# A two-layer diffusion step in one kernel: the opening's scale and shift vectors from TensorE in column groups, six tiles from the scaled, un-normalised input

## The chip, the core and the metric

The kernel runs on one core of a Trainium2 chip. Its engines work side by side, each on its own queue of instructions in order: TensorE (PE in the profile; its weight loads are PEld), VectorE (DVE), ScalarE (ACT), GpSimd (POOL) and SyncE (SP), which issues the loads. Transfers are carried by 16 DMA engines. The metric is the device time of one execution in microseconds; the median of several runs is compared.

## The reference

One inference step of a two-layer backbone over 384 tokens of width 1024: 128 context tokens (modulated by `c_ctx`) and 256 latent tokens (modulated by `c`). Each layer is a half-step SwiGLU FFN, a token mixer (layer 0: a bidirectional recurrent block, layer 1: grouped-query attention) and a second half-step FFN. Each of these reads a normalised and modulated input. What the change touches is the input of the very first FFN:

```python
def rmsnorm(x, g):
    y = xf * lax.rsqrt(jnp.mean(xf * xf, axis=-1, keepdims=True) + EPS)
    return (y * g).astype(x.dtype)

def modulation(cvec, w, b):
    m = jax.nn.silu(cvec) @ w + b
    return m.reshape(cvec.shape[0], N_SUB, 3, D_MODEL)

def sub_in(x, g, m, sidx):
    shift, scale = m[:, sidx, 0], m[:, sidx, 1]
    return rmsnorm(x, g[sidx]) * (1 + scale[:, None, :]) + shift[:, None, :]

def swiglu(h, w_gu, w_down):
    gt, up = jnp.split(h @ w_gu, 2, axis=-1)
    return (jax.nn.silu(gt) * up) @ w_down
...
xs = xs + 0.5 * sub_gate(ms, 0) * swiglu(sub_in(xs, g, ms, 0), ffn_w_gu[layer, 0], ffn_w_down[layer, 0])
```

Since the norm's factor is one number per token, `(x * r * G + S) @ W` equals `r * ((x * G) @ W) + S @ W`, with `G = (1 + scale) * g` and `S` the shift. A product can therefore start from `x * G` without the norm, if `S @ W` is computed beside it and `r` is multiplied in afterwards.

## The kernel before

**Layout.** Activations lie transposed: 8 blocks (k = 0 to 7) of 128 features on the partitions, 384 tokens along the row (128 context, then 256 latent). Each float32 operand is split into a high part (a rounded copy, `hi`, usually made on ScalarE, line 162) and a low part (the rest, `lo`, made on VectorE, line 163), and each product is three matmuls: hi by hi, hi by lo, lo by hi (`mm3`, lines 173 to 178). `hh` and `hl` (lines 101 to 103) hold the two parts of the current input, with two more columns 384 and 385 (`N:NB`) for the two shift vectors; `ALL` is 384 columns, `AUG` 386. A weight tile is 128 output features by all 1024 inputs, 512 KB, and takes 8 x 3 matmuls.

**Later sub-layers** already use the identity above: `pre` writes `x * G`, `shift_cols` writes the shift columns, `head` runs six tiles on 386 columns, and `ev` in `ffn` (lines 400 to 412) multiplies the norm `R` in and adds the shift product taken from columns 384 and 385. Then `hgen` (line 313) writes the truly normalised input for the other tiles.

**The opening** (`start`, line 993) is the exception. It loads the small constants and the input `X`, spreads the two conditioning vectors over all partitions with eight matmul instructions (line 1016) into `sb`, squares `X` for the norm's statistics (`square`, line 270), and loads for each k the scale tile (`sc`), the shift tile (`sh`) and one of six gate/up weight tiles (`GUP`). All of these loads are issued from SP. Then a list of tokens, `SPROG` (line 68), writes out the order of the work:

- `A`: the scale vector of k = 0 and the statistics; `N`: the norm, spread into `R` (`norm_end`).
- `S`k: the shift of k < 6 on TensorE: eight matmuls against `sT` (two columns) into two PSUM rows, and a copy of them to `row` (lines 1037 to 1045). `T`k: a turn of that row into a column, by a small matmul, and its bias on ScalarE. For k = 6 and 7 the shift is computed by two dots on VectorE instead (`mod_dot`, line 196: one pass over 128x1024 elements for each conditioning vector).
- `H`k (`gen`): the scale of k by two dots on VectorE, then `hgen`, the normalised input of block k.
- `P`k (`step`): the matmuls that block k makes possible for the six tiles, on 384 columns.

Three things fix the order. All matmuls of `start` that go through its `mm` are chained ("pe"), so TensorE takes them in the order of SPROG. On VectorE the dots and the low parts of the six weight tiles are chained ("fill"); other operations are placed by a scheduler where it finds room. And in a pool of buffers a load waits until the buffer before it is free: `mc` (scale and shift tiles) has 12, `gr` (the six raw weight tiles) 6, `raw` (later weights) 3.

After `start`, `ffn` evacuates the six tiles in three pairs (`evac`, line 394), and goes on with ordinary tiles (`plain`, line 379, whose matmuls appear at lines 175 to 177) on the normalised input. These are not chained.

Of the kernel before, what the change touches and what calls it, by code (L numbers as in the profile page):

```python
# [37 lines left out]
MP = 0  # L38
# [24 lines left out]
XO = [slice(0, 4), slice(4, 8)]  # L63
SHP = 6
CP = ()
GUP = (0, 1, 2, 3, 4, 5)
PB = True
SPROG = "A S0 N S1 T0 H0 S2 T1 H1 P0 S3 T2 H2 P1 S4 T3 H3 P2 S5 T4 H4 P3 T5 H5 P4 P5 T6 H6 T7 H7 P6 P7"
# [18 lines left out]
class Net:  # L87
# [98 lines left out]
    def mod_pe(self, l, n):  # L186
        nc = self.nc
        raw = self.wp.tile([P, 1024], F32, tag="raw", name="raw", bufs=3)
        nc.sync.dma_start(raw, self.a["mod_w"][l, n])
        ps = self.misc()  # L190
        for k in range(KD):
            nc.tensor.matmul(ps[:, :2], lhsT=raw[:, k * P:(k + 1) * P], rhs=self.sT[:, k, :], start=k == 0, stop=k == KD - 1)
        st, k = divmod(n, KD)
        nc.vector.tensor_copy(self.mod[l, st // 3, st % 3][:, k, :], ps[:, :2])

# [91 lines left out]
    def stats(self):  # L287
        nc = self.nc
        ps = self.misc()
        st = ps[:, N:]  # L290
        for i in range(3):
            c = slice(i * P, (i + 1) * P)
            self.chain("pe", nc.tensor.matmul(st[:, i:i + 1], lhsT=self.acc[:, c], rhs=self.ones[:, 0:1], start=True, stop=True))
        self.nps, self.ny = ps, self.rstd(st[:, :3], 3, 1.0 / D)
# [90 lines left out]
    def ffn(self, l, s, fills, nxt, banks=None, hp=3, begun=None, prep=False):  # L385
# [607 lines left out]
    def start(self, B=6):  # L993
# [3 lines left out]
        sh, sc = {}, {}  # L997
        row = {}
        one = T_([P, KD], F32, name="one")
        if PB:  # L1000
            cr = self.fp.tile([P, 1024], F32, tag="junk", name="junk", bufs=1)[0:2, :]
            sel = T_([2, 2, P], F32, name="sel")
            nc.sync.dma_start(cr, a["cv"])
            nc.sync.dma_start(sel, a["sel"])
# [6 lines left out]
        if PB:
            nc.scalar.activation(cr, cr, AF.Silu)
            for v in range(2):
                for c in (slice(0, 512), slice(512, 1024)):
                    b = self.bank()
                    nc.tensor.matmul(b, lhsT=sel[:, v, :], rhs=cr[:, c], start=True, stop=True)
                    nc.scalar.activation(self.sb[:, v, c], b, AF.Copy)
        else:
            self.load_cond()
        for k in range(KD):  # L1020
            self.square(k)
        nc.vector.tensor_scalar(out=one, in0=self.sm("mod_b", KD, KD), scalar1=1.0, scalar2=None, op0=ALU.add)
        los = []
        banks = [self.bank() for _ in range(B)]
        tr = self.bank()
        tiles = []
        for k in range(KD):
            for o, dst in ((KD, sc), (0, sh)):
                dst[k] = T_([P, D], F32, tag="mc", name="mc", bufs=12)
                nc.sync.dma_start(dst[k], a["mod_w"][0, o + k])  # L1030
            for _ in range(GUP.count(k)):
                tiles.append(self.gu_tile(0, 0, len(tiles), T_([P, D], F32, tag="gr", name="gr", bufs=B)))
                los.append(self.wlo)
        self.last["pe"] = None
        S, G = self.mod[0, 0, 0], self.mod[0, 0, 1]

        def shift(k, src=None):
            if src is None:
                if k >= SHP:
                    return  # L1040
                src = sh[k]
            for j in range(KD):
                mm(tr[0:2, :P], lhsT=self.sT[:, j, :], rhs=src[:, j * P:(j + 1) * P], start=j == 0, stop=j == KD - 1)
            row[k] = T_([2, P], F32, tag="row", name="row", bufs=3)
            nc.scalar.activation(row[k], tr[0:2, :P], AF.Copy)

        def turn(k):
            if k >= SHP:
                self.mod_dot(0, k, sh[k])
                nc.vector.tensor_scalar(out=S[:, k, :], in0=S[:, k, :], scalar1=self.sm("mod_b", k, 1), scalar2=None, op0=ALU.add)  # L1050
                return
            mm(tn[:, 2 * k:2 * k + 2], lhsT=row[k], rhs=self.ident[0:2, 0:2], start=True, stop=True)
            nc.scalar.activation(S[:, k, :], tn[:, 2 * k:2 * k + 2], AF.Identity, bias=self.sm("mod_b", k, 1))

        def scale(k):
            if k in CP:
                return
            self.mod_dot(0, KD + k, sc[k])
            scale_end(k, G[:, k, :])

        def scale_pe(k):
            mm(tn[:, 64 + 2 * k:64 + 2 * k + 2], lhsT=row[k], rhs=self.ident[0:2, 0:2], start=True, stop=True)
            scale_end(k, tn[:, 64 + 2 * k:64 + 2 * k + 2])

        def scale_end(k, src):
            g = self.sm("norm_g", k, 1).to_broadcast([P, 2])
            nc.vector.scalar_tensor_tensor(out=G[:, k, :], in0=src, scalar=one[:, k:k + 1], in1=g, op0=ALU.add, op1=ALU.mult)
# [13 lines left out]
        def gen(k):  # L1081
            if k:
                scale(k)
            for i in range(B):
                if GUP[i] == k:
                    self.chain("fill", los[i])
            keep = self.last["fill"]
            self.hgen(0, 0, k)
            self.last["fill"] = keep

        def first():
            self.last["fill"] = None
            scale(0)
            self.stats()

        def second():
            self.norm_end()
            self.last["fill"] = self.dg

        tn = None  # L1100
        for tok in SPROG.split():
            k = int(tok[1:] or 0)
            if tok[0] in "TD" and tn is None:
                tn = self.misc()
            {"S": lambda: shift(k), "C": lambda: shift(k, sc[k]), "D": lambda: scale_pe(k), "T": lambda: turn(k), "H": lambda: gen(k), "P": lambda: step(k),
             "A": first, "N": second}[tok[0]]()
# [5 lines left out]
    def run(self):  # L1112
        self.nst = self.res.tile([P, 16], F32, name="nst")
        self.fillq = [(0, n) for n in range(16, 72) if MP == 0 or n // KD != 7] + [(1, n) for n in range(72)]
# [119 lines left out]
```

## Time and profile before

| | us |
|---|---|
| median of 3 runs (1422.58 to 1427.07) | 1426.04 |
| the profiled execution's own time | 1420.91 |
| its span, first to last instruction | 1419.0 |
| first load issued | 0.72 |
| the eight spreading matmul instructions, start and busy time | 3.41, 7.19 |
| first matmul of the six opening tiles | 24.52 |
| last matmul of the six opening tiles starts | 65.26 |
| mean granted TensorE clock (1 is full speed) | 0.996 |

The page gives shares of one profiled execution. The prediction below goes from the page to the stretches of the opening, then to single rows. In a timeline row stand the start, the length, the engine, the line, the operation, what it writes and reads, and in brackets how long the engine had been idle before and what released it. A matmul's length in such a row overlaps with its neighbours; the price of a stream of matmuls is read from their starts, or from the chain of waits.

### The profile page before, as it was taken

The numbers are of one execution on the slowest core, as the hardware profiler recorded it, in microseconds if no ns is written. First come the engines' busy times: TensorE is split into PE (matmuls) and PEld (weight loads), VectorE is DVE, ScalarE is ACT, GpSimd is POOL, SyncE is SP. The second block draws the span as 40 slices with busy tenths as digits, with TensorE's granted clock in tenths as the row PEclk, the third lists the DMA queues.
The fourth block names the chain that finished last, engine by engine and source line by source line (L and its number), as shares of the span: only waits on it lengthen the run. The fifth ranks groups of instructions, "written<-read, shape, count | busy, mean of one in ns | idle before, by whom it ended". The sixth has DMA issues, their size and how long they took to land.

```text
span 1419.0 us, 21055 instructions
## 1 busy us (share of the span) xinstructions
PE 1388.8 (98%) x8020; PEld 1363.3 (96%) x8020; DVE 1072.8 (76%) x1942; ACT 651.1 (46%) x1067; POOL 23.2 (2%) x32
## 2 busy tenths in 40 slices
PE   7999999999998999999999999999998999999997
PEld 4999999999888999999999999999998999999997
DVE  7799989977987898879858887897797765444331
ACT  5443433339995643333345333333676554333221
POOL 0000000000110000000000000000000000000110
PEclk9999999999999999999999999999999999999999
DMA  9377777762135387767726766675330324334431
GB/s 373 132 252 252 228 226 247 239 206 90 60 119 178 124 260 224 218 199 245 231 73 198 247 210 205 219 245 178 105 112 31 118 90 150 133 121 125 123 93 45
DMA packets 69516, 245.67 MB, mean 173 GB/s; under 512 B 7844, under 2 KB 8486, under 8 KB 69416
## 3 DMA queue, kind: packets, MB, share of 16 engines
q1 hardware_dynamic: 69416, 244.34, 52.8%
q8 instruction: 63, 1.03, 0.3%
q14 instruction: 37, 0.30, 0.1%
HBM read 242.46 MB, written 1.84 MB: 172 GB/s over the span
## 4 chain that ended last, share of the span: by engine, by line
PE 91%; DVE 3%; ACT 3%; DMA 1%; issue 1%; SPq 0%; DVEq 0%; ACTq 0%
PE b L177 26%; PE b L175 26%; PE b L176 25%; PE b L749 5%; PE b L504 5%; PE b L995 2%; PE m L749 1%; ACT rrt L507 1%; ACT ttt L507 1%; DMA sb<-in_cv 0%; DVE lo L163 0%; DVE lo L511 0%; ACT L507 0%; DMA raw<-in_lru_w_out 0%; DVE ttt L511 0%
## 5 line engine op out<-in xcount | busy, mean ns | idle before, releaser
L162 ACT ACTIVATE hi<-raw 128x1024 fp32r<-128x1024 f32 (+1 forms) x284 | 293.8, 1036 | 600.9 <-issue 321.6
L177 PE MATMUL b<-hh,lo 128*128 128x384 f32 (+1 forms) x1372 | 461.9, 337 | 0.0
L175 PE MATMUL b<-hh,hi 128*128 128x384 f32 (+1 forms) x1372 | 460.6, 337 | 0.0
L176 PE MATMUL b<-hh,hi 128*128 128x384 f32 (+1 forms) x1372 | 456.7, 333 | 0.0
L163 DVE TENSOR_TENSOR lo<-raw,hi 128x1024 fp32r<-128x1024 f32 (+1 forms) x284 | 338.2, 1192 | 135.9 <-ACT hi L162 132.5
L202 DVE CUSTOM_DVE_ANT_0 junk<-mraw,sb 128x1024 f32<-128x1024 f32 x256 | 312.2, 1219 | 5.3 <-DMA mraw<-in_mod_w 2.6
L176 PEld LDWEIGHTS b<-hh,hi 128*128 128x128 f32 x1372 | 258.2, 188 | 0.0
L177 PEld LDWEIGHTS b<-hh,lo 128*128 128x128 f32 x1372 | 257.6, 188 | 0.0
L175 PEld LDWEIGHTS b<-hh,hi 128*128 128x128 f32 x1372 | 257.4, 188 | 0.0
L175 PE MATMUL b<-hid,hi 128*128 128x384 f32 x704 | 235.2, 334 | 0.0
L176 PE MATMUL b<-hid,hi 128*128 128x384 f32 x704 | 235.2, 334 | 0.0
L177 PE MATMUL b<-hid,lo 128*128 128x384 f32 x704 | 235.2, 334 | 0.0
L176 PEld LDWEIGHTS b<-hid,hi 128*128 128x128 f32 x704 | 132.2, 188 | 0.0
L177 PEld LDWEIGHTS b<-hid,lo 128*128 128x128 f32 x704 | 132.2, 188 | 0.0
L175 PEld LDWEIGHTS b<-hid,hi 128*128 128x128 f32 x704 | 132.2, 188 | 0.0
L397 DVE TENSOR_TENSOR t<-t,b 128x384 f32<-128x384 f32 x79 | 43.5, 551 | 72.7 <-PE b L177 72.7
L504 PE MATMUL b<-hh,hi 128*128 128x386 f32 x328 | 88.4, 350 | 4.0 <-DVE X L511 3.9
L504 PEld LDWEIGHTS b<-hh,hi 128*128 128x128 f32 x328 | 60.7, 192 | 7.2 <-issue 3.7
L346 DVE SCALAR_TENSOR_TENSOR X<-b,m,X 128x128 f32<-128x128 f32 x80 | 29.6, 412 | 42.3 <-PE b L177 36.6
L504 PE MATMUL b<-hh,lo 128*128 128x386 f32 x164 | 56.1, 342 | 0.0
L170 ACT ACTIVATE hid<-t 128x384 fp32r<-128x384 f32 x88 | 45.2, 514 | 9.0 <-DVE t L397 8.4
L171 DVE TENSOR_TENSOR hid<-t,hid 128x384 fp32r<-128x384 f32 x88 | 48.4, 550 | 0.0
(208 smaller groups left out, 1332.5 us busy)
## 6 DMA issues: line engine op xcount, KB each, us to landing
raw<-in_gu SPq DMA_DIRECT2D x170, 512.0 KB, 4.0
mraw<-in_mod_w SPq DMA_DIRECT2D x128, 512.0 KB, 4.2
raw<-in_down SPq DMA_DIRECT2D x64, 512.0 KB, 3.7
raw<-in_down SPq DMA_DIRECT2D x32, 384.0 KB, 4.3
mc<-in_mod_w SPq DMA_DIRECT2D x16, 512.0 KB, 10.2
raw<-in_lru_w_in SPq DMA_DIRECT2D x16, 512.0 KB, 3.3
raw<-in_w_qkv SPq DMA_DIRECT2D x10, 512.0 KB, 3.3
raw<-in_lru_w_out SPq DMA_DIRECT2D x8, 512.0 KB, 3.4
```

What stands on the lines that cost most here:

```text
L162: nc.scalar.activation(hi[:, :cols], raw[:, :cols], AF.Copy)
L163: self.wlo = nc.vector.tensor_tensor(out=lo[:, :cols], in0=raw[:, :cols], in1=hi[:, :cols].bitcast(F32), op=ALU.subtract)
L170: self.nc.scalar.activation(hi, src, AF.Copy)
L171: return self.nc.vector.tensor_tensor(out=lo, in0=src, in1=hi.bitcast(F32), op=ALU.subtract)
L175: first = mm(out, lhsT=lh, rhs=rh, start=start, stop=False)
L176: mm(out, lhsT=lh, rhs=rl, start=False, stop=False)
L177: self.end = mm(out, lhsT=ll, rhs=rh, start=False, stop=stop)
L202: i = nc.vector.tensor_tensor_reduce(out=junk, in0=raw, in1=self.sb[:, v, :], scale=1.0, scalar=0.0, op0=ALU.mult, op1=ALU.add, accum_out= ...
L346: self.nc.vector.scalar_tensor_tensor(out=x, in0=b[:, GRP[g]], scalar=self.mod[l, s, 2][:, m, g:g + 1], in1=x, op0=ALU.mult, op1=ALU.add)
L397: nc.vector.tensor_tensor(out=x, in0=x, in1=bu[:, ALL], op=ALU.mult)
L504: return self.chain("pe", nc.tensor.matmul(*args, **kw))
L749: return self.chain("pe", T.matmul(*args, **kw)) if PIN else T.matmul(*args, **kw)
```

## The change

`start` is rewritten, and the six tiles are taken over by `ffn` in the manner of the later sub-layers.

- The scale vectors of all eight k, and the shifts of k = 4, 6 and 7 (`SPE`), are computed on TensorE. `sT` is widened to 32 columns per block (30 of them zero), and the eight matmuls of a vector go to four groups of 32 PSUM partitions. The copy `row` is then 128x128, and the turn is a matmul of it against a constant `sel4` that adds the four groups.
- The shifts of k = 0, 1, 2, 3 and 5 are two dots each on VectorE.
- The six tiles read `x * G` (`gen`: high part on ScalarE, low part on VectorE) and the shift columns, 386 columns in all. VectorE's operations of `start` for one k are chained: scale, low parts, low parts of the weight tiles that join at this k, shift dots, split of the shift columns.
- Two of the six tiles join at k = 0, one each at 1 and 2, two at 3 (`GUP`). The token `X` is the statistics, `N` the norm, `L` the last two blocks of all six tiles, tile by tile.
- Loads are issued in the order of `LOADS`, `X` in four pieces instead of two.
- In `ffn` the normalised input of k = 0 to 5, the three evacuations with norm and shift (`ev`), and the normalised input of k = 6 and 7 follow.
- The host lays out the tiles that TensorE takes accordingly. Unused switches and `mod_pe` go.

```diff
-SHP = 6
-GUP = (0, 1, 2, 3, 4, 5)
-SPROG = "A S0 N S1 T0 H0 S2 T1 H1 P0 S3 T2 H2 P1 S4 T3 H3 P2 S5 T4 H4 P3 T5 H5 P4 P5 T6 H6 T7 H7 P6 P7"
+SPE = (4, 6, 7)
+GUP = (0, 0, 1, 2, 3, 3)
+LOADS = "x0 c0 g0 s0 g1 c1 s1 g2 x2 c2 s2 g3 c3 s3 g4 g5 x4 c4 s4 c5 s5 x6 c6 s6 c7 s7"
+SPROG = "C0 T0 H0 C1 P0 T1 H1 C2 P1 T2 H2 C3 P2 X T3 H3 C4 S4 P3 T4 U4 H4 C5 P4 N T5 H5 C6 S6 P5 T6 U6 H6 C7 S7 T7 U7 H7 L"
...
         elif banks:
-            for j in range(hp):
-                evac(j, *banks[2 * j:2 * j + 2])
+            for k in range(KD - 2):
+                self.hgen(l, s, k)
+            for i in range(2 * hp):
+                ev(i, banks)
+            for k in range(KD - 2, KD):
+                self.hgen(l, s, k)
...
+        sT = T_([P, KD, 32], F32, name="sT")
+        nc.gpsimd.memset(sT, 0.0)
...
+        def rows(t):
+            r = slice(len(row) % 4 * P, len(row) % 4 * P + P)
             for j in range(KD):
-                mm(tr[0:2, :P], lhsT=self.sT[:, j, :], rhs=src[:, j * P:(j + 1) * P], start=j == 0, stop=j == KD - 1)
+                q = slice((j % 4) * 32, (j % 4) * 32 + 32)
+                mm(tr[q, r], lhsT=sT[:, j, :], rhs=got[t][:, j * P:(j + 1) * P], start=j < 4, stop=j >= 4, skip_group_check=True)
+            row[t] = T_([P, P], F32, tag="row", name="row", bufs=2)
+            nc.scalar.activation(row[t], tr[:, r], AF.Copy)
+
+        def turn(t):
+            o = 400 + 2 * int(t[1]) + (32 if t[0] == "s" else 0)
+            mm(tn[:, o:o + 2], lhsT=row[t], rhs=sel4, start=True, stop=True, skip_group_check=True)
+            return tn[:, o:o + 2]
 
         def scale(k):
-            self.mod_dot(0, KD + k, sc[k])
-            scale_end(k, G[:, k, :])
+            fill(nc.vector.scalar_tensor_tensor(out=G[:, k, :], in0=turn(f"c{k}"), scalar=one[:, k:k + 1], in1=g,
+                                                op0=ALU.add, op1=ALU.mult))
+
+        def shift(k):
+            nc.scalar.activation(S[:, k, :], turn(f"s{k}"), AF.Identity, bias=self.sm("mod_b", k, 1))
+
+        def gen(k):
+            for g in range(2):
+                x, z = self.X[:, k, GRP[g]], G[:, k, g:g + 1]
+                hi = self.hh[:, k, GRP[g]]
+                nc.scalar.activation(hi, x, AF.Copy, scale=z)
+                fill(nc.vector.scalar_tensor_tensor(out=self.hl[:, k, GRP[g]], in0=x, scalar=z, in1=hi.bitcast(F32),
+                                                    op0=ALU.mult, op1=ALU.subtract))
+            for i in range(B):
+                if GUP[i] == k:
+                    fill(los[i])
+            if k not in SPE:
+                self.mod_dot(0, k, got[f"s{k}"])
+                fill(nc.vector.tensor_scalar(out=S[:, k, :], in0=S[:, k, :], scalar1=self.sm("mod_b", k, 1), scalar2=None, op0=ALU.add))
+            fill(self.split(self.hh[:, k, N:NB], self.hl[:, k, N:NB], S[:, k, :]))
 
         def pair(k, i):
...
-                mm(banks[i][:, ALL], lhsT=lh[:, c], rhs=rh[:, k, ALL], start=k == 0 and n == 0, stop=k == KD - 1 and n == 2)
+                mm(banks[i][:, AUG], lhsT=lh[:, c], rhs=rh[:, k, AUG], start=k == 0 and n == 0, stop=k == KD - 1 and n == 2)
...
+        def last():
             for i in range(B):
+                for k in (KD - 2, KD - 1):
+                    pair(k, i)
+
+        ops = {"C": lambda k: rows(f"c{k}"), "S": lambda k: rows(f"s{k}"), "T": scale, "U": shift, "H": gen, "P": step}
+        rest = {"X": lambda: self.stats(tn), "N": self.norm_end, "L": last}
```

More of the change, by code (lines that the diff above doesn't have):

```diff
@@ L184, in mmk @@
         return self.mm3(out, w[0][:, c], w[1][:, c], xh[:, k, cols], xl[:, k, cols], start, stop)
[L186 to L194, printed above, removed]
     def mod_dot(self, l, n, raw):
@@ L996, in start @@
         T_ = self.ph.tile
-        sh, sc = {}, {}
-        row = {}
+        got, row, tiles, los = {}, {}, [], []
         one = T_([P, KD], F32, name="one")
[L1000 to L1004, printed above, removed]
+        cr = self.fp.tile([P, 1024], F32, tag="junk", name="junk", bufs=1)[0:2, :]
+        sel = T_([2, 2, P], F32, name="sel")
@@ L1011, in start @@
[L1011 to L1019, printed above, removed]
+        nc.scalar.activation(sT[:, :, 0:2], self.sm("cvec").rearrange("p (k v) -> p k v", v=2), AF.Silu)
@@ new lines, in start @@
+        nc.scalar.activation(cr, cr, AF.Silu)
+        for v in range(2):
+            for c in (slice(0, 512), slice(512, 1024)):
+                b = self.bank()
+                nc.tensor.matmul(b, lhsT=sel[:, v, :], rhs=cr[:, c], start=True, stop=True)
+                nc.scalar.activation(self.sb[:, v, c], b, AF.Copy)
+        nc.vector.tensor_scalar(out=one, in0=self.sm("mod_b", KD, KD), scalar1=1.0, scalar2=None, op0=ALU.add)
+        banks = [self.bank() for _ in range(B)]
+        tr, tn = self.bank(), self.misc()
@@ new lines, in start @@
+        for tok in LOADS.split():
+            c, k = tok[0], int(tok[1])
+            if c == "x":
+                nc.sync.dma_start(self.X[:, k:k + 2, :], a["x"][:, k:k + 2, :])
+            elif c == "g":
+                tiles.append(self.gu_tile(0, 0, k, T_([P, D], F32, tag="gr", name="gr", bufs=B)))
+                los.append(self.wlo)
+            else:
+                got[tok] = T_([P, D], F32, tag="mc", name="mc", bufs=12)
+                nc.sync.dma_start(got[tok], a["mod_w"][0, k + (KD if c == "c" else 0)])
@@ L1020, in start @@
         for k in range(KD):
             self.square(k)
[L1022 to L1033, printed above, removed]
@@ L1047, in turn @@
[L1047 to L1053, printed above, removed]
-        def scale(k):
-            if k in CP:
-                return
-            self.mod_dot(0, KD + k, sc[k])
-            scale_end(k, G[:, k, :])
@@ L1061, in scale_pe @@
[L1061 to L1065, printed above, removed]
-            g = self.sm("norm_g", k, 1).to_broadcast([P, 2])
-            nc.vector.scalar_tensor_tensor(out=G[:, k, :], in0=src, scalar=one[:, k:k + 1], in1=g, op0=ALU.add, op1=ALU.mult)
+        self.last["pe"] = self.last["fill"] = None
+        S, G = self.mod[0, 0, 0], self.mod[0, 0, 1]
@@ new lines, in start @@
+        fill = lambda i: self.chain("fill", i)
+        def rows(t):
+            r = slice(len(row) % 4 * P, len(row) % 4 * P + P)
+            for j in range(KD):
+                q = slice((j % 4) * 32, (j % 4) * 32 + 32)
[6 more added lines that the diff above has]
+            return tn[:, o:o + 2]
@@ L1079, in step @@
                         pair(j, i)
-        def gen(k):
-            if k:
-                scale(k)
+        def last():
             for i in range(B):
[L1085 to L1100, printed above, removed]
-        for tok in SPROG.split():
[L1102 to L1106, printed above, removed]
+                for k in (KD - 2, KD - 1):
+                    pair(k, i)
+        ops = {"C": lambda k: rows(f"c{k}"), "S": lambda k: rows(f"s{k}"), "T": scale, "U": shift, "H": gen, "P": step}
+        rest = {"X": lambda: self.stats(tn), "N": self.norm_end, "L": last}
+        for tok in SPROG.split():
+            if tok in rest:
+                rest[tok]()
+            else:
+                ops[tok[0]](int(tok[1:]))
         return banks
@@ L1113, in run @@
         self.nst = self.res.tile([P, 16], F32, name="nst")
-        self.fillq = [(0, n) for n in range(16, 72) if MP == 0 or n // KD != 7] + [(1, n) for n in range(72)]
+        self.fillq = [(0, n) for n in range(16, 72)] + [(1, n) for n in range(72)]
         with self.filling():
@@ L1176 @@
     mod = np.ascontiguousarray(mw.transpose(0, 2, 1).reshape(2, NTM, P, D))
[L1177 to L1181 removed]
+    for n in SPE + tuple(range(KD, 2 * KD)):
+        mod[0, n] = wtiles(mw[0, :, n * P:(n + 1) * P])[0]
     h["mod_w"] = mod
```

31 lines of the change are left out of this document (9 added, 22 removed).

## The prediction

> **What bounds the kernel now.** I read the page first: its span, the busy shares, and the shares of the chain of waits.
>
> ```profile
> span 1419.0 us, 21055 instructions
> PE 1388.8 (98%) x8020; PEld 1363.3 (96%) x8020; DVE 1072.8 (76%) x1942; ACT 651.1 (46%) x1067; POOL 23.2 (2%) x32
> PE 91%; DVE 3%; ACT 3%; DMA 1%; issue 1%; SPq 0%; DVEq 0%; ACTq 0%
> ```
>
> TensorE is 98% busy and carries 91% of the chain. So the opening is worth what it changes in one thing: when the matmul stream becomes gapless, and how many matmuls are behind it then. I read that from busy time by stretch (columns: stretch, length, then busy time of PE, PEld, DVE, ACT, POOL, granted clock, DMA share, GB/s).
>
> ```profile
> 10.00:20.00 10.00, 7.53 (x42) 5.07 (x42) 9.13 (x26) 4.19 (x7) 0.00 (x0) 1.00 1.03 411
> 20.00:30.00 10.00, 5.93 (x36) 3.58 (x34) 10.00 (x21) 5.76 (x11) 0.00 (x0) 0.89 1.03 410
> 30.00:40.00 10.00, 10.00 (x67) 7.92 (x66) 10.00 (x19) 5.16 (x11) 0.00 (x0) 0.94 1.03 408
> 40.00:50.00 10.00, 10.00 (x60) 9.47 (x58) 7.78 (x15) 3.82 (x9) 0.00 (x0) 1.00 0.38 138
> 60.00:120.00 60.00, 60.00 (x348) 60.00 (x347) 53.02 (x77) 27.96 (x39) 0.00 (x0) 1.00 0.70 230
> ```
>
> From 10 to 40 us VectorE is full and so are the DMA engines (about 410 GB/s). From 30 us on TensorE is full and stays so. The chain in order of time (start, length, what) gives the point:
>
> ```profile
> 25.61 1.14 DVE lo L163
> ...
> 27.02 0.48 DVE hh L171
> 27.54 4.06 PE b L995 x18
> ```
>
> Until 27.5 us the end hangs on VectorE; from there on TensorE. The last matmul of the six opening tiles (line 995) is followed by ordinary ones (lines 175 to 177) at 65.43, and 8 + 7 + 7 = 22 of those had been slipped in between by then (timeline of TensorE, then the three lines' own busy time by stretch):
>
> ```profile
> 65.26 0.34 PE L995 MATMUL b<-hh,lo 128*128 128x384 f32 x1
> 65.43 0.33 PE L176 MATMUL b<-hh,hi 128*128 128x384 f32 x1
> ...
> 27.50:65.10 37.60, 2.69 (x8) 1.50 (x8) 0.95 0.44 172
> 27.50:65.10 37.60, 2.33 (x7) 1.31 (x7) 0.95 0.44 172
> 27.50:65.10 37.60, 2.36 (x7) 1.31 (x7) 0.95 0.44 172
> ```
>
> 60 us hold 348 matmuls, 0.172 us each, so 22 are 3.8 us. Without them the six tiles' 144 matmuls would have been done at 65.4 - 3.8 = **61.6 us**. That is the mark to beat: behind it every stage is TensorE's.
>
> **The order on the engines decides this change.** Matmuls of the opening are chained in the order of SPROG. The trace keeps it to the letter: S3, T2, P1, S4, T3, P2.
>
> ```profile
> 27.54 0.55 PE L995 MATMUL b<-hh,hi 128*128 128x384 f32 x1 [2.58 <-DVE hh L171]
> ...
> 28.34 3.26 PE L995 MATMUL b<-mc,sT 128*2 128x128 f32 x16
> 31.53 0.38 PE L995 MATMUL m<-ident,row 2*128 2x2 f32 x2
> ...
> 33.61 1.91 PE L995 MATMUL b<-mc,sT 128*2 128x128 f32 x16
> 35.44 0.38 PE L995 MATMUL m<-ident,row 2*128 2x2 f32 x2
> ```
>
> In the kernel before, VectorE needs nothing from TensorE to go on (its scale dots read loads), so it runs ahead. In the new order T1 stands behind P0, T2 behind P1, and so on. Each T makes the scale column that VectorE's next chained operation reads; and each P reads 386 columns, the last two being the shift column, which for k = 0, 1, 2, 3, 5 comes from two dots at the end of VectorE's chain for that k. So P(k) waits for VectorE's whole step k, and VectorE's step k+1 waits for P(k): the two engines take turns. Behind the waiting P stand T and all later opening matmuls; behind the waiting scale stand the products, splits and dots of that k. What can fill VectorE's waits is not chained (sums of squares, the norm, later weight splits), and TensorE has no other work, as ordinary tiles need the normalised input, made last.
>
> **The price of one step.** Groups by line and shape within the first 66 us (count | busy, mean ns | idle before):
>
> ```profile
> L202 DVE CUSTOM_DVE_ANT_0 junk<-mc,sb 128x1024 f32<-128x1024 f32 x20 | 24.4, 1218 | 0.1
> L163 DVE TENSOR_TENSOR lo<-gr,hi 128x1024 fp32r<-128x1024 f32 x6 | 7.3, 1218 | 0.0
> L1067 DVE SCALAR_TENSOR_TENSOR m<-m,one,small 128x2 f32<-128x2 f32 x8 | 1.7, 216 | 0.1
> L1045 ACT ACTIVATE row<-b 2x128 f32<-2x128 f32 x6 | 1.6, 264 | 8.7 <-PE b L995 8.7
> L1053 ACT ACTIVATE m<-m,small 128x2 f32<-128x2 f32 x6 | 1.6, 258 | 2.5 <-PE m L995 2.3
> L323 ACT ACTIVATE hh<-t,m 128x256 fp32r<-128x256 f32 x2 | 1.0, 504 | 0.0
> L324 DVE SCALAR_TENSOR_TENSOR hh<-t,m,hh 128x256 fp32r<-128x256 f32 x2 | 1.0, 478 | 0.0
> L323 ACT ACTIVATE hh<-t,m 128x128 fp32r<-128x128 f32 x2 | 0.8, 404 | 6.1 <-DVE t L319 6.1
> L324 DVE SCALAR_TENSOR_TENSOR hh<-t,m,hh 128x128 fp32r<-128x128 f32 x2 | 0.7, 346 | 0.0
> ```
>
> - Turn 0.38, scale 0.22, two high parts on ScalarE 0.40 + 0.50, the second low part 0.48 (the first lies beside ScalarE), handovers about 0.1: **2.1 us**.
> - Each weight split chained to that k: **1.2 us** (two at k = 0 and 3, one at 1 and 2; the high part is done earlier on ScalarE).
> - Two dots, each 1.22 and a read-out: **2.5 us**; where the shift comes from TensorE instead (k = 4, 6, 7), none.
> - Bias and split of the shift column, three tiny operations at the price of lines 1067 and 1053: **0.75 us** (0.5 where ScalarE adds the bias).
>
> So k = 0: 2.1 + 2.4 + 2.5 + 0.75 = 7.75; k = 1 and 2: 6.55 each; k = 3: 7.75; k = 4: 2.6; k = 5: 5.35. Together **36.55 us** in which no opening tile advances.
>
> **Before and between.** The first scale rows (C0) stand behind the eight matmuls that spread the conditioning vectors, which end at 10.6; their input is now issued second, so about 11.0. The next rows give the rows' cold price and two landings.
>
> ```profile
> 3.41 7.19 PE L1016 MATMUL b<-junk,sel 2*128 2x512 f32 x8 [3.41 <-ACT junk L1012]
> ...
> 12.17 1.06 ACT L162 ACTIVATE hi<-gr 128x1024 fp32r<-128x1024 f32 x1 [0.85 <-DMA gr<-in_gu]
> ...
> 14.41 3.39 PE L995 MATMUL b<-mc,sT 128*2 128x128 f32 x16
> ...
> 16.02 1.06 ACT L162 ACTIVATE hi<-gr 128x1024 fp32r<-128x1024 f32 x1 [2.79 <-DMA gr<-in_gu]
> ```
>
> Sixteen row instructions cost 3.39 us early and 1.91 later. Whether the eight matmuls of a row, now in four column groups, run side by side, the trace cannot show: between a quarter of the row (0.85) and the whole 3.39. I take the whole, the row itself, and keep the quarter for the range. T0 then stands at 11.0 + 3.4 + 0.3 (copy) = **14.7 us**.
>
> Loads don't hold this up. Three 512 KB loads lie between the two landings at 12.17 and 16.02, 1.28 us each. The last x pair comes 12 loads later than the second of them, at 31.4, the last shift tile at 36.5; by the steps above they are wanted at 42 and beyond 70. The order of loads, whatever it does on SP's queue, is worth nothing here (prefetches of later weights slipped in ahead of the last four cost 1.28 each, under the same cover).
>
> Matmul work between the steps: P0 to P5 have 6, 12, 18, 36, 18, 18 = 108 matmuls of 386 columns; X and N are three statistics and three spreads. Their price from the chain where such matmuls run later:
>
> ```profile
> 315.10 0.56 PE m L293 x6
> ...
> 460.15 0.67 PE m L266 x6
> 460.81 3.73 PE b L504 x21
> ```
>
> 108 x 0.178 = 19.2 us, and 0.56 + 0.67 = 1.2 us. (The two added columns cost 0.005 us each time, inside this.) P5 ends at 14.7 + 36.55 + 19.2 + 1.2 = **71.65 us**.
>
> The tail: T6, U6 (0.7), rows C7 and S7 (2 x 1.91), copy 0.3, then step 7 of 2.6: 7.4 us. L's 36 matmuls are 6.4 us, of which 0.5 (tile 0, k = 6) lies inside the wait. End of the six tiles: 71.65 + 7.4 + 6.4 - 0.5 = **85.0 us**, against 61.6: **+23.4 us**.
>
> Edits taken at nothing: VectorE loses ten dots (12.2 us) and gains eight pairs of low parts (some 6.6 us by line 324) and, as an estimate from lines 324 and 1067, about 5 us of small column operations and longer evacuations: net about nothing; the eight normalised inputs move behind the steps. After L the first ordinary tiles have 18 matmuls (3.1 us) each for k = 0 to 5, which cover the last two normalised inputs. If that cover is too thin, up to 3 us are added: VectorE first has three evacuations to do. Statistics on VectorE could slip into step 3's chain: 0 to 2 us. Memsets and small loads lie in front of 11 us, beside the spreading matmuls.
>
> The profiled execution took 1420.9 us (1419.0 span), under the median of 1426.0. 1420.9 + 23.4 = 1444.3 as a profiled run; on the median, which I predict, **1449 us**.
>
> **The rivals.**
> - *Column groups run side by side*: C0 costs a quarter (2.5 less), C7 and S7 together 2.8 less: +18 us, **1444**. For it: the groups write separate partitions. Against: no row shows it. In the Trainium skill, TensorEngine Tiling (Array Packing), section Theoretical Speedup, a small dimension of at most 32 allows up to 4x; no run here shows that yet.
> - *TensorE is slow after each wait*: after its idle 2.58 us the sixteen row instructions at 28.34 took 3.26 us against 1.91 at 33.61, 1.35 more, and the granted clock of 20 to 30 us is 0.89. P0, P1, P2, P3, P5 and L would each follow a wait longer than 2.58: 6 x 1.35 = 8.1 us more, **1457**. Against: rows run inside the waits. The Trainium skill, TensorE: Matmul & The Clock Gate, Part 1, says that an idle window of about 3.4 us halves the clock until a busy one has passed, which speaks against a design with such waits; the slow row agrees in kind.
> - *Faster*: the taking of turns doesn't happen, because the scale turns overtake the P's or the shift columns come early. Then the loads bind: last tile at 36.5, rows, turn and step 7 of some 4 us, L 6.4: 47, so 14.6 less, **1411**. It decides if the gap between P(k) and P(k+1) falls under about 2.5 us for most k. For it: VectorE's whole work up to L, some 36 us, would fit beside the loads. Against: the order quoted above is kept strictly.
> - *Half-way*: the steps overlap so far that end and mark meet, within 4 us of **1426**.
>
> **How the numbers follow.** The likeliest case, turns with rows at full price, 0.45; side by side 0.15; slow after waits 0.22; half-way 0.07; faster 0.10; something worse (an engine queue blocked by a load) 0.01. A measurement of this kernel can tell about 0.3% from no change. So slower 0.83, same 0.07, faster 0.10. The range, 1435 to 1462, reaches from the shared columns with some 9 us of steps overlapped to the slow clock with the thin cover; it leaves out the faster and half-way cases.
>
> **What would show it.** Right: on TensorE, waits of 5 to 8 us before the first matmul of P0 to P3 and P5, released by VectorE's tiny split of the shift column; VectorE idle during P3; DMA engines quiet long before L; the six tiles' last matmul between 79 and 95 us. Wrong: gapless matmuls before 40 us, or VectorE full through 45 us. If rows of one k last under 1 us when warm, the column groups do share.

## The result, and the profile after

The changed kernel takes **1462.69 us** (median of 4 runs, 1460.40 to 1465.44); the kernel before, run beside it on the same chip, 1425.15. The ratio is 1.0259, with a 95% interval of 1.0240 to 1.0279: 37.5 us slower. The prediction was slower by 23.4, at 1449, with a range up to 1462. So the direction was right, the size was 14 us too small, and the time lies just above the range. The profiled execution took 1463.67 us, its span 1461.7.

The page of the changed kernel, its span, TensorE's busy time and the engines' shares of the chain of waits:

```profile
span 1461.7 us, 21299 instructions
PE 1396.8 (96%) x8110; PEld 1372.3 (94%) x8110; DVE 1072.0 (73%) x1964; ACT 658.0 (45%) x1096; POOL 25.1 (2%) x33
PE 90%; ACT 4%; DVE 4%; DMA 1%; issue 1%; DVEq 0%; ACTq 0%; SPq 0%
```

TensorE's busy time grew by 8.0 us (1388.8 before), the span by 42.7. So most of the loss is TensorE standing still, and a part of it is TensorE working longer. Busy time by stretch shows where (stretch, length, then busy time of PE, PEld, DVE, ACT, POOL, granted clock, DMA share, GB/s):

```profile
20.00:30.00 10.00, 3.52 (x24) 3.02 (x24) 6.76 (x15) 4.94 (x9) 0.00 (x0) 1.00 1.03 408
30.00:40.00 10.00, 4.88 (x30) 4.52 (x30) 5.45 (x14) 2.94 (x7) 0.00 (x0) 0.91 1.03 409
40.00:50.00 10.00, 7.16 (x58) 6.52 (x58) 4.06 (x16) 1.28 (x5) 0.00 (x0) 0.74 0.26 102
50.00:60.00 10.00, 4.19 (x12) 3.79 (x13) 6.33 (x16) 0.37 (x2) 0.00 (x0) 0.60 0.17 52
60.00:70.00 10.00, 9.14 (x61) 8.76 (x60) 1.22 (x4) 1.32 (x5) 0.00 (x0) 0.89 0.01 2
70.00:80.00 10.00, 3.13 (x45) 2.38 (x44) 7.68 (x19) 6.63 (x17) 0.00 (x0) 0.79 0.00 0
80.00:90.00 10.00, 7.00 (x56) 6.43 (x56) 3.71 (x11) 2.88 (x10) 0.00 (x0) 0.70 0.00 0
```

Before, TensorE was full from 30 us on. Now it is half empty up to 60, VectorE is never full either, and where TensorE is nearly full VectorE hardly works (60 to 70), and where VectorE works most TensorE is at its emptiest (70 to 80): the two take turns. The loads, which went on to 43 us before, are over at about the same time but for one, long before the tiles. And the granted clock, 0.94 or more from 30 us on before, falls to 0.60.

The waits of the first 101 us (engine, line, releaser: us in total, times, longest):

```profile
PE b L986 <- ACT hh L167: 31.8, 6, 7.8
DVE m L1042 <- PE m L986: 29.2, 6, 9.2
ACT hh L167 <- DVE m L1060: 17.6, 5, 5.4
```

Line 986 is the helper that issues all matmuls of the opening, 167 the high part of the shift column, 1042 the scale, 1060 the bias of the shift that VectorE's dots made. The matmuls wait for the shift column, it waits for the dots' bias, and VectorE's scale waits for TensorE's turn. This is the circle that the prediction drew. Its one half, the 31.8 us in which the matmuls wait, lies inside the steps that were forecast at 36.55 in all; its other half is the 29.2 us in which VectorE waits for a turn. The chain in order of time gives the steps (start, length, what, count). The 6, 12, 18, 36, 18 and 18 matmuls are P0 to P5, the 36 at the end are L:

```profile
14.20 0.60 PE m L986 x2
...
22.33 2.30 PE b L986 x6
...
30.91 4.18 PE b L986 x12
...
41.62 4.99 PE b L986 x18
...
55.81 9.66 PE b L986 x36
...
67.41 3.44 PE b L986 x18
...
82.29 5.16 PE b L986 x18
...
93.77 6.74 PE b L986 x36
...
347.01 3.72 PE b L495 x21
```

The last row is a landmark: the 21 matmuls with which the recurrent block opens, which stand in the kernel before at

```profile
311.38 3.72 PE b L504 x21
```

So the stages between the opening and there carry the loss on unchanged: **35.6 us** are lost in the opening (the six tiles end at 100.35; without the 18 ordinary matmuls, 3.1 us, that ran in ahead of L, at 97.2, against the mark of 61.6). I use this landmark below, as it is free of what varies behind it. From the landmark to the end of their time, the profiled executions of this study took between 1109.5 us (before) and 1117.5 (one of the experiments), though no edit touches those stages; the profiled execution of the kernel before was the quickest of all there. That is why the span grew by 42.7 and the median only by 37.5.

### The profile page after: what moved, and what is told of

Read it like the earlier page. It is cut to its first block, busy times and chain, and to the rows that moved or that the text cites. A ratio compares the mean times of both kernels' runs of the same rounds, so it can differ in the third digit from the quotient of the medians.

```text
span 1461.7 us, 21299 instructions
## 1 busy us (share of the span) xinstructions
PE 1396.8 (96%) x8110; PEld 1372.3 (94%) x8110; DVE 1072.0 (73%) x1964; ACT 658.0 (45%) x1096; POOL 25.1 (2%) x33
## 4 chain that ended last, share of the span: by engine, by line
PE 90%; ACT 4%; DVE 4%; DMA 1%; issue 1%; DVEq 0%; ACTq 0%; SPq 0%
PE b L174 25%; PE b L172 25%; PE b L173 24%; PE b L740 5%; PE b L495 5%; PE b L986 3%; PE m L740 1%; DVE junk L189 1%; DVE lo L160 1%; ACT rrt L498 1%; ACT ttt L498 1%; PE b L1006 0%; DMA sb<-in_cv 0%; PE b L876 0%; ACT L498 0%
## 5 line engine op out<-in xcount | busy, mean ns | idle before, releaser
L173 PEld LDWEIGHTS b<-hh,hi 128*128 128x128 f32 x1372 | 258.1, 188 | 0.0
L172 PEld LDWEIGHTS b<-hh,hi 128*128 128x128 f32 x1372 | 257.3, 188 | 0.2 <-ACT row L1033 0.2
L495 PE MATMUL b<-hh,hi 128*128 128x386 f32 x328 | 89.8, 354 | 7.0 <-DVE X L502 5.2
L495 PEld LDWEIGHTS b<-hh,hi 128*128 128x128 f32 x328 | 61.6, 195 | 10.5 <-issue 5.8
L986 PE MATMUL b<-hh,hi 128*128 128x386 f32 x96 | 32.8, 429 | 31.8 <-ACT hh L167 31.8
L986 PEld LDWEIGHTS b<-hh,hi 128*128 128x128 f32 x96 | 22.9, 247 | 34.5 <-ACT hh L167 34.0
```

The lines of the kernel that those rows point to most:

```text
L172: first = mm(out, lhsT=lh, rhs=rh, start=start, stop=False)
L173: mm(out, lhsT=lh, rhs=rl, start=False, stop=False)
L495: return self.chain("pe", nc.tensor.matmul(*args, **kw))
L986: mm = lambda *args, **kw: self.chain("pe", nc.tensor.matmul(*args, **kw))
```

## The experiments

All of them, by the landmark in the profiled execution and by the median. "Ratio" is against the kernel before, run beside them (1425.15 to 1427.25).

| kernel | landmark, us | later than before | median, us | ratio (95%) |
|---|---|---|---|---|
| changed kernel | 347.01 | +35.6 | 1462.69 | 1.0259 (1.0240 to 1.0279) |
| turns ahead of the matmuls | 325.31 | +13.9 | 1441.15 | 1.0108 (1.0089 to 1.0128) |
| all shifts on TensorE | 330.21 | +18.8 | 1444.45 | 1.0124 (1.0106 to 1.0142) |
| twelve idle matmuls per wait | 346.38 | +35.0 | 1457.47 | 1.0223 (1.0196 to 1.0251) |
| waits filled with idle matmuls | 338.54 | +27.2 | 1454.06 | 1.0190 (1.0172 to 1.0209) |
| normalised input late | 345.77 | +34.4 | 1459.97 | 1.0235 (1.0215 to 1.0254) |
| filled waits and input late | 336.60 | +25.2 | 1450.05 | 1.0156 (1.0139 to 1.0173) |
| one column group | 352.21 | +40.8 | 1468.14 | one run |
| loads of X first | 347.00 | +35.6 | 1458.87 | one run |
| turns two steps ahead | 325.24 | +13.9 | 1436.74 | 1.0077 (1.0055 to 1.0100) |
| turns ahead, five shifts on TensorE | 325.58 | +14.2 | 1437.86 | 1.0088 (1.0070 to 1.0107) |
| before, shifts in column groups | 311.51 | +0.1 | 1426.89 | 0.9999 (0.9987 to 1.0010) |
| before, and three scales in groups | 310.87 | -0.5 | 1425.58 | 0.9997 (0.9985 to 1.0010) |

**Is it the order?** Each turn T(k+1) with the rows that feed it goes ahead of P(k), so VectorE's step k+1 no longer waits for P(k):

```diff
-SPROG = "C0 T0 H0 C1 P0 T1 H1 C2 P1 T2 H2 C3 P2 X T3 H3 C4 S4 P3 T4 U4 H4 C5 P4 N T5 H5 C6 S6 P5 T6 U6 H6 C7 S7 T7 U7 H7 L"
+SPROG = "C0 T0 H0 C1 T1 H1 P0 C2 T2 H2 P1 C3 T3 H3 P2 X C4 S4 T4 U4 H4 P3 C5 T5 H5 P4 N C6 S6 T6 U6 H6 P5 C7 S7 T7 U7 H7 L"
```

> Every turn T(k+1) (and its rows) stands ahead of P(k) in the order on TensorE; nothing else changes. Taking of turns: VectorE then runs its chained steps one behind the other from 14 us (8.1 + 5.9 + 5.9 + 7.1 + 1.9 + 4.8 + 2 x 1.9 = 37.5), the P's lie beside them, the six tiles end near 58 us instead of 97, and the kernel takes about 1424 us (39 less than the changed kernel). Rival, the slow clock alone: about 9 less, 1454. Rival, VectorE's list is simply too long whatever the order: under 5 less, 1458 or more.

21.7 us of the 35.6 go, so the order is the larger part of the loss. It fell short of the 39 that were expected. One wait of the old kind is left: T5 stands behind P3's 36 matmuls, and VectorE with nothing chained to do waits for it:

```profile
52.20 0.22 DVE L1042 SCALAR_TENSOR_TENSOR m<-m,one,small 128x2 f32<-128x2 f32 x1 [5.98 <-PE m L986]
```

It isn't what held the end: the kernel with turns two steps ahead, below, no longer has this wait and ends at the same time.

**All shifts on TensorE**, with the turns left behind the P's as in the change. This takes the two dots, 2.5 us, out of the steps of k = 0, 1, 2, 3 and 5:

```diff
-SPE = (4, 6, 7)
+SPE = (0, 1, 2, 3, 4, 5, 6, 7)
-SPROG = "C0 T0 H0 C1 P0 T1 H1 C2 P1 T2 H2 C3 P2 X T3 H3 C4 S4 P3 T4 U4 H4 C5 P4 N T5 H5 C6 S6 P5 T6 U6 H6 C7 S7 T7 U7 H7 L"
+SPROG = "C0 S0 T0 U0 H0 C1 S1 P0 T1 U1 H1 C2 S2 P1 T2 U2 H2 C3 S3 P2 X T3 U3 H3 C4 S4 P3 T4 U4 H4 C5 S5 P4 N T5 U5 H5 C6 S6 P5 T6 U6 H6 C7 S7 T7 U7 H7 L"
```

> The changed kernel with all eight shifts on TensorE (rows S, turn U), no dots on VectorE in the opening; the taking of turns stays. Theory: steps 0, 1, 2, 3 and 5 lose two dots each, 2.5 us: 12 us less, and one or two more where shorter waits leave the clock up: 1447 to 1451 us. Rival, the dots lie beside other work: no change, 1462. Rival, the added rows and turns on TensorE cost what they did before (1.9 us a row): 2 less only, 1460.

16.8 us go by the landmark, more than the five pairs of dots (12.2) and more than was expected. A part of the surplus is the price of the matmuls: P1 and P2, with no long wait before them, take 3.1 and 3.6 us instead of 4.0 and 4.8. The loss can thus be attacked at either end of the circle: TensorE's turns earlier, or less work for VectorE in a step.

**Is it the clock?** Twelve 128x128 matmuls on constants, which nothing reads, stand in the waits before P0, P1, P2, P3 and P5 (token Z):

```diff
+        def warm(k):
+            for _ in range(12):
+                mm(tn[:, 0:P], lhsT=self.ones, rhs=self.ones, start=True, stop=True, skip_group_check=True)
...
-SPROG = "C0 T0 H0 C1 P0 T1 H1 C2 P1 T2 H2 C3 P2 X T3 H3 C4 S4 P3 T4 U4 H4 C5 P4 N T5 H5 C6 S6 P5 T6 U6 H6 C7 S7 T7 U7 H7 L"
+SPROG = "C0 T0 H0 C1 Z0 P0 T1 H1 C2 Z1 P1 T2 H2 C3 Z2 P2 X T3 H3 C4 S4 Z3 P3 T4 U4 H4 C5 P4 N T5 H5 C6 S6 Z5 P5 T6 U6 H6 C7 S7 T7 U7 H7 L"
```

> The changed kernel with 12 more 128x128 matmuls of ones into an unused stretch of PSUM, results not used, in each of the waits before P0, P1, P2, P3 and P5. If the slow clock after the waits costs what the P's lengths show (2.1 + 4.0 + 4.8 + 9.5 + 5.0 us against 1.1 + 2.1 + 3.2 + 6.4 + 3.2), these P's come back to about 1.1, 2.1, 3.2, 6.4 and 3.2: some 9 us less, 1453 us. If the P's are long for another reason (waits inside them), nothing changes: 1462. If the added matmuls outlast the waits, a few us more.

By the median some 5 of the 9 us came, but the landmark moved by 0.6 only: of the 5.1 us between the two profiled executions 4.5 lie behind it, where the edit doesn't reach. Twelve leave 1.4 to 2.9 us of each wait empty. Its chain:

```profile
22.29 1.34 PE b L986 x6
29.45 3.47 PE b L986 x12
...
54.25 8.00 PE b L986 x35
...
79.11 6.16 PE b L986 x18
...
89.05 0.32 PE b L172
```

P0, P1 and P3 are faster by 0.7 to some 1.4 us (P3's piece holds 35 of its 36), P5 is slower by 1.0, and the ordinary matmuls behind it (line 172) now take 0.32 us each instead of 0.17: the low clock was moved, not removed. This left the question open, so the waits were filled to the end, 10, 20, 20, 24 and 28 instead of twelve:

> The changed kernel with idle matmuls as in the run with twelve of them, but as many as fill the waits: 10 before P0, 20 before P1 and P2, 24 before P3, 28 before P5. Theory (the lower clock behind the waits is the idle time's doing): P0 to P5 take 1.1, 2.1 to 2.6, 3.3 to 3.8, 6.4 to 7 and 3.2 to 4 us instead of 2.1, 4.0, 4.8, 9.5 and 5.0, the tiles end 7 to 9 us earlier than in the changed kernel, 1453 to 1456. Rival (the clock falls by what the first 100 us draw, not by idle time, or the chip's clock falls behind any fp32 burst): the P's stay where twelve left them (1.17, 3.27, 4.9, 8.5, 5.95) and the time is 1457 or more.

The chain, and two stretches of busy time:

```profile
22.28 1.77 PE b L986 x6
...
30.49 2.10 PE b L986 x12
...
38.77 3.65 PE b L986 x18
...
52.30 6.42 PE b L986 x35
...
75.53 3.45 PE b L986 x18
...
40.00:50.00 10.00, 9.01 (x94) 8.45 (x93) 6.76 (x18) 1.24 (x4) 0.00 (x0) 1.00 0.26 100
50.00:60.00 10.00, 8.95 (x67) 8.23 (x65) 2.75 (x12) 1.08 (x4) 0.00 (x0) 1.00 0.17 52
```

P0, P1, P2, P3 and P5 together take 17.4 us (again with 35 of P3's 36) instead of 26.3, the granted clock is 1.00 where it was 0.74 and 0.60, and the landmark comes 8.5 us earlier, the median 8.6. The same matmuls on the same data at the same places in the order: their price hung on whether TensorE had stood still before them. The rivals, that the clock falls by what the opening draws or behind any burst of fp32 matmuls, fall: there is more TensorE work here, and the clock is up. A short stop is enough, though: ten idle matmuls left 2.3 us of the wait ahead of P0, and its last three matmuls fell to half speed (1.77 us for the six, where 0.178 each would be 1.1).

**What lengthens step 5?** T5 to P5 took 10.18 us against 5.35 predicted. VectorE in that stretch of the changed kernel:

```profile
72.08 1.03 DVE L314 TENSOR_TENSOR t<-X,R 128x384 f32<-128x384 f32 x2 [4.53 <-ACT R L286]
...
74.62 0.21 DVE L1042 SCALAR_TENSOR_TENSOR m<-m,one,small 128x2 f32<-128x2 f32 x1
...
78.43 1.22 DVE L189 CUSTOM_DVE_ANT_0 junk<-mc,sb 128x1024 f32<-128x1024 f32 x1
...
79.57 1.02 DVE L168 TENSOR_TENSOR hh<-t,hh 128x384 fp32r<-128x384 f32 x2
```

The norm (R) is ready at 72.08, and from then on the normalised input of the ordinary tiles can be made. It isn't chained, so it goes ahead of the scale of k = 5 (74.62) and in between its dots. The experiment orders its first operation for k = 0 to 5 behind the last chained one of the opening:

```diff
         elif banks:
+            self.after = self.last["fill"]
             for k in range(KD - 2):
                 self.hgen(l, s, k)
+            self.after = None
...
+    def late(self, ins):
+        if self.after is not None:
+            self.tc.add_manual_dep(ins.ins, self.after.ins.name,
+                                   mybir.DependencyInfo(mybir.DependencyClass.NoSync, mybir.DependencyReason.DATA),
+                                   reason="order")
+        return ins
```

> The changed kernel with VectorE's first operation of each normalised input of k = 0 to 5 ordered behind the last chained operation of the opening. Theory: these operations stretched step 5 from 5.3 to 10.2 us by slipping in ahead of its scale and between its dots; step 5 falls to about 5.5 us, and of the 4.7 us saved up to 3 come back after L, where the normalised inputs are now late: 0 to 5 less, 1458 to 1463. Rival, they only filled VectorE's idle time: no change in step 5.

Timeline of TensorE, T5 and the first matmuls of P5:

```profile
71.33 0.38 PE L996 MATMUL m<-sel,row 128*128 128x2 f32 x2 [0.58 <-ACT R L287]
...
76.30 1.01 PE L996 MATMUL b<-hh,hi 128*128 128x386 f32 x2 [2.62 <-ACT hh L168]
```

The step takes 4.97 us. But only 1.2 us reach the landmark (2.7 the median): no ordinary matmuls are ready to run in the tail's waits, and behind L the first of them waits for its input. The work that had got in the way was needed soon after.

**Do the two terms add?** Both edits together, with 10, 20, 20, 24 and 8 idle matmuls:

> The changed kernel with both of the terms put back that the prediction had mis-sized: idle matmuls in the waits (10, 20, 20, 24 and 8) and the ordinary tiles' input chain behind the last scale. Theory (the two account for what lies between 1449 as predicted and 1462.7 as measured, and they add): 8.6 us from the clock and 2.7 from the order, so 1451.4, within 1449 to 1454, with T5 to P5 at about 5 us and P5 at 3.2. Rival (both recover the same slack: what the one frees, the other no longer can): the time stays at the 1454.1 of the kernel with the idle matmuls alone, or above.

1450.05, ratio 1.0156 (1.0139 to 1.0173), 23.7 us above the kernel before it ran beside: what had been predicted for the change itself. Its chain at step 5 and its landmark, and the first ordinary matmul that waits behind L (timeline):

```profile
66.06 0.40 PE m L996 x2
...
71.02 3.44 PE b L996 x18
...
336.60 3.72 PE b L505 x21
...
87.20 0.44 PE L174 MATMUL b<-hh,hi 128*128 128x384 f32 x1 [1.73 <-DVE hh L169]
```

L is over at 84.8 there, where the prediction had 85.0. That the two meet this closely is partly luck: the P's are still 1.7 us and X and N 1.2 above the prediction's price, tail and L 2.8 below it. The landmark is 25.2 us late and the tiles 23.2, as 1.7 us more are lost in that wait behind L.

**Column groups.** The eight matmuls of a row, in one group of 32 PSUM partitions instead of four; all else as in the change:

```diff
-                q = slice((j % 4) * 32, (j % 4) * 32 + 32)
-                mm(tr[q, r], lhsT=sT[:, j, :], rhs=got[t][:, j * P:(j + 1) * P], start=j < 4, stop=j >= 4, skip_group_check=True)
+                q = slice(0, 32)
+                mm(tr[q, r], lhsT=sT[:, j, :], rhs=got[t][:, j * P:(j + 1) * P], start=j == 0, stop=j == KD - 1, skip_group_check=True)
...
-            nc.scalar.activation(row[t], tr[:, r], AF.Copy)
+            nc.scalar.activation(row[t][0:32, :], tr[0:32, r], AF.Copy)
```

> The changed kernel with the eight matmuls of a row all on one group of 32 PSUM partitions, adding up there; copy and turn on those 32 partitions. If column groups run side by side, a row's sixteen instructions go back from 1.08 (early) and 0.64 us to about 3.4 and 1.9; most lie inside waits, so the kernel loses 3 to 6 us (C0, and C7 with S7). If the groups were not what shortens them, they stay at 1.08 and 0.64 and the time stays.

TensorE's rows in the timeline: two of the changed kernel, then two with one group.

```profile
12.72 1.08 PE L986 MATMUL b<-mc,sT 128*32 128x128 f32 x16
...
35.14 0.64 PE L986 MATMUL b<-mc,sT 128*32 128x128 f32 x16
```

```profile
12.77 3.62 PE L986 MATMUL b<-mc,sT 128*32 128x128 f32 x16
...
38.26 1.93 PE L986 MATMUL b<-mc,sT 128*32 128x128 f32 x16
```

The groups run side by side: 3.35 times faster early, 3.0 times at full clock. They are worth 5.2 us of the landmark here.

**The order of loads**: all of X ahead of the other loads (`LOADS = "x0 x2 x4 x6 c0 g0 s0 g1 ..."`).

> The changed kernel with all four pieces of X loaded first. Theory: loads do not bind, since every step of this opening comes after its load has landed; step times stay within 1 us and the time within 3 us. Rival, the order of loads matters: C0's tile lands 2.9 us later and each step moves back by that much.

The landmark stands at 347.00, where the changed kernel has 347.01; the 4 us that the single time is lower lie behind it. So at the landmark the loads' order is worth nothing, as the prediction had it, but the equality is luck. P5 starts 2.4 us earlier (82.29 in the changed kernel):

```profile
79.91 1.01 PE L986 MATMUL b<-hh,hi 128*128 128x386 f32 x2 [7.78 <-ACT hh L167]
```

1.7 us of it are shorter steps of k = 0 to 4: the sums of squares (0.47 each), of which five stand in VectorE's chain in the changed kernel, are done earlier. Then P5 and the 18 ordinary matmuls behind it run at half speed for longer and use the gain up (5.8 us instead of 5.0, and 4.8 instead of 3.2).

**Is there a good version of the idea?** Turns two steps ahead at the large P3 (T4 and T5 before P3, T6 before P4, T7 before P5, N behind H7):

> As e1_turns_first, but from k = 4 on the turns run further ahead: T4 and T5 before P3, T6 before P4, T7 before P5, and the norm N after H7. Theory: in e1 VectorE still stood idle behind P3 (its scale of k = 5 waited 6 us for a turn queued behind the 36 matmuls), so taking of turns was only half undone; now P3 to P5 and L follow each other with only rows and turns between, and the six tiles end near 69 us instead of 75.5 (18 ordinary matmuls taken off): about 6 less than e1, 1435. Rival, VectorE's list binds: the same end as e1, 1441.

and, the other way, one step ahead but with the shifts of k = 0, 1, 2, 5 and 7 on TensorE (`SPE = (0, 1, 2, 5, 7)`):

> Turns ahead as in e9, and the shifts of k = 0, 1, 2, 5 and 7 on TensorE (dots for 3, 4 and 6). Theory: both engines' lists are then about even, P0 starts near 20 us, P3 near 34, the six tiles end near 60 us, where the kernel before has them at 61.6: 1422 to 1430, no slower than the kernel before by more than 0.3%. Rival, the loads or the slow clock bind in this stretch: 1435 or more.

Both end where the first reordering did, 14 us behind the kernel before by the landmark; their medians are 1436.7 and 1437.9. The chain of the first shows why:

```profile
43.96 0.56 PE m L986 x2
...
46.57 8.63 PE b L986 x52
...
65.41 10.20 PE b L986 x54
```

Until 44 us its chain runs through VectorE's and ScalarE's steps of k = 0 to 3 with hardly a gap, and only then come the matmuls that those steps hold up. The circle is gone, but VectorE's own work is now on the path. What follows is no gapless stream either: from 44 us to the tiles' end at 75.4 TensorE has 108 matmuls, 19.2 us at the prediction's price; the rest is rows, copies, turns and the norm between them, and matmuls below full speed (P3 with the sixteen row instructions behind it takes 8.63 us, where 36 x 0.178 + 0.64 would be 7.0). In the second, turns and scales get in each other's way: a turn writes columns of the PSUM buffer whose other columns VectorE's last scale still reads, and it is released by that scale, after 2.71 us and then 4.09 (timeline of TensorE, the later one):

```profile
46.33 0.56 PE L986 MATMUL m<-sel,row 128*128 128x2 f32 x2 [4.09 <-DVE m L1042]
```

That the shared buffer, and not another wait ending at the same time, causes this was not tried.

**Are the column groups worth something alone?** In the kernel before, the six shift rows in four groups, with the turn against `sel4`, and nothing else of the change:

```diff
+            r = slice(len(used) % 4 * P, len(used) % 4 * P + P)
+            used.append(k)
             for j in range(KD):
-                mm(tr[0:2, :P], lhsT=self.sT[:, j, :], rhs=src[:, j * P:(j + 1) * P], start=j == 0, stop=j == KD - 1)
-            row[k] = T_([2, P], F32, tag="row", name="row", bufs=3)
-            nc.scalar.activation(row[k], tr[0:2, :P], AF.Copy)
+                q = slice((j % 4) * 32, (j % 4) * 32 + 32)
+                mm(tr[q, r], lhsT=sT[:, j, :], rhs=src[:, j * P:(j + 1) * P], start=j < 4, stop=j >= 4, skip_group_check=True)
+            row[k] = T_([P, P], F32, tag="row", name="row", bufs=2)
+            nc.scalar.activation(row[k], tr[:, r], AF.Copy)
```

> The kernel before, with nothing of the change but its column groups: the six shift rows run as four side by side groups of 32 columns, and their turns add the four rows up. Theory (the groups are the one part that is worth something): TensorE has no wait from 31.8 us on in the kernel before, and behind its P0 stand the rows of S3 (3.26), S4 (1.91) and S5 (1.91); at the 1.08 and 0.64 that the changed kernel's rows took they give back 2.2 + 1.3 + 1.3 = 4.7 us, so about 1420.5, the mark 57 instead of 61.6. Rival (VectorE, busy 10.00 of 10 from 20 to 40 us, or the loads, which end at 43 us, bind there and TensorE only waits more): the mark moves by less than 1 us and the time is within 0.3% of before.

Nothing: 0.9999 (0.9987 to 1.0010). The rows are shorter, but the chain of waits, which in the kernel before came over to TensorE at 27.54, now names loads and then VectorE until 45.17:

```profile
28.85 9.17 DMA raw<-in_gu
...
44.65 0.48 DVE hh L171
...
45.17 0.96 PE b L995 x4
```

VectorE is busy 9.97 us of the ten from 30 to 40 there and 9.67 of the next ten, so P4 waits for VectorE's own list; that the loads bind as well isn't shown. The list also began later, with its first scale dot at 12.53 instead of 11.22. And TensorE lost on its matmuls a part of what it saved on rows: P1's nine took 3.3 us instead of 1.7. So the row time had been cover for VectorE, and the run can't say what the groups would be worth with VectorE's list as early as before. The scales of k = 1, 2 and 3 on TensorE as well (`CP = (1, 2, 3)`, with tokens C and D for their rows and turns put in ahead of H1 to H3):

> As the one before it, and the scale vectors of k 1, 2 and 3 on TensorE too (three more sets of rows and three turns), which takes six dots of 1.22 us off VectorE between 18 and 35 us. If VectorE binds the first three steps, P0 to P2 start 2 to 4 us earlier than in the kernel with the groups alone, and the time is 1417 to 1420; if the loads bind, it is the same as there (within 1 us); if the order of TensorE's turns behind ScalarE's copies costs more than the dots did, it is slower by 1 to 3 us.

It gives 0.5 us at the landmark and no difference in time, 0.9997 (0.9985 to 1.0010). Here neither VectorE (busy 5.29 us of the ten from 40 to 50) nor the loads hold the end; the chain is TensorE's without a gap from 31.1 us on:

```profile
31.10 5.20 PE b L995 x41
```

In front of that stand the rows, copies and turns that were added, and P1's nine matmuls, in this piece, again take 3.2 us. No version that I tried beats the kernel before.

## Why the prediction came out as it did

**What held.** The circle of waits: steps of 5 to 10 us, released by the split of the shift column, VectorE idle during P3 (9.2 us), loads quiet from 43 us on. That TensorE's gapless start is what counts: 35.6 us lost there arrive in full at the recurrent block. That the order of loads is worth nothing at the landmark, though with luck, as shown above. And the forecast of slower, at 0.83.

**What failed.** By the prediction's own terms, with the kernel that has both terms put right (filled waits, input late) beside them; starts of T0, P, T, X and N in the timeline of TensorE (by the six tiles the prediction is 12.2 us short, by the median 14.1):

| term, us | predicted | changed kernel | both put right |
|---|---|---|---|
| T0 | 14.7 | 14.2 | 14.0 |
| steps k0 to k4 | 31.2 | 31.8 | 32.0 |
| step k5 | 5.35 | 10.2 | 5.0 |
| P0 to P5 | 19.2 | 28.7 | 20.9 |
| X and N | 1.2 | 2.4 | 2.4 |
| tail and L | 13.3 | 9.9 | 10.5 |
| end of the six tiles | 85.0 | 97.2 | 84.8 |

- **The price of the P's is the step that failed**, "108 x 0.178 = 19.2 us": +9.5. The price came from a stretch where TensorE never stops (460.81, 21 matmuls in 3.73), and was used behind waits of 5 to 8 us, where the first matmuls ran at 0.32. The rival "TensorE is slow after each wait" had the mechanism and, with 8.1 us, nearly the size, but I gave it 0.22, with the argument that rows run inside the waits: they stand at the start of the wait and are over 5 us before its end. The Trainium skill (TensorE: Matmul & The Clock Gate, Part 1) has half the clock after an idle window of about 3.4 us. The runs agree for the waits of 5 to 8 us, which were followed by matmuls at about half speed, while those of under 1 us ahead of P2, P3 and P5, in the kernel with filled waits, were not. But they show half speed behind shorter waits too: behind 2.62 us, ahead of P5 with the input late, the first two matmuls took 1.01 us, as they did behind 7.77 in the changed kernel. The rule should have changed the term, not been left to a rival.
- **Step 5**: +4.8. I counted the normalised input as moved "behind the steps", because it is written there. It isn't chained, so its place was wherever VectorE was free after N.
- **Rows at full price**: they share, 0.64 instead of 1.91. The rival had this at 5.3 us and 0.15; one group instead of four costs 5.2. The tail's 3.4 us less hold its share of that, and 18 ordinary matmuls that ran inside the tail's waits. At T0 little of it shows (14.2 against 14.7), because the spreading matmuls, taken to end at about 11.0, ended at 12.7.
- **X and N**: +1.2, their handovers to VectorE and ScalarE weren't priced.
- **The bound before** was read as TensorE from 27.5 us on. It was, but with VectorE close behind: its last operation for H2 ended at 35.51, 0.24 us before TensorE came to P2, and the one for H4 at 43.56, 1.3 us before P4. With TensorE's rows cut in the kernel before, the end didn't move.
- **The range** reached to the slow clock "with the thin cover", but not to the slow clock and a longer step 5 together; that is what happened, less the sharing.

Had the P's been priced as they ran (9.5 more) and the rows as shared (5.3 less), the sum would have been 23.4 + 9.5 - 5.3 = 27.6, so 1453.6; step 5 would still have been missing.

## What to carry to other kernels

Before a chain is written out by hand, look for a circle in it: if engine A's step needs B's result and B's next step is queued behind A's, their times add, however well each is filled alone. Price matmuls by what stands right before them: the same instruction costs nearly twice as much behind a wait of some microseconds, so a wait is paid twice, and idle matmuls that filled it gave 8.5 us of that back here. And where one engine's list ends just behind another's, relieving the first buys little: in the kernel before, work taken off TensorE turned up as a wait for VectorE, and work taken off VectorE as more work on TensorE.

## What the runs showed of the hardware

- Idle matmuls that fill 3 us of a 5 us wait don't keep the clock up; the matmuls behind start fast and fall to half speed 1 to 2 us later (the chain with twelve: P1 3.47 us for 12 matmuls, against 2.10 with the wait filled). The clock answers late, to what went before.
- Longer rows may have had a use. In the kernel before, 3.26 us of rows at 28.34 were followed by P1's nine matmuls in 1.7 us. With the rows in groups, 1.08 us at 27.25, the nine took 3.3 us, though no wait in the 10 us before them exceeded 1.5 us. With all shifts on TensorE, P0's six took 2.1 us, with no wait above 1.3 us in the 10 us before. So short stops and small matmuls don't always keep the clock up. Each is read from one profiled execution, and that the longer rows were the reason wasn't tested.
- Sixteen fp32 row instructions of 32 columns cost 3.62 us in one column group and 1.08 in four at the low clock, 1.93 and 0.64 at the full one. The Trainium skill (TensorEngine Tiling (Array Packing), Theoretical Speedup) allows up to 4x for a dimension of at most 32; here it is 3.0 to 3.35.
- The granted clock reads 1.00 from 20 to 30 us of the changed kernel, where matmuls ran at half speed (P0, six in 2.30 us). So early in this trace the column cannot be trusted, and durations of a known instruction are the better clock.
